# Output projection and MLP of an encoder trunk: the instruction order of VectorE, ScalarE and GpSimd written by hand instead of left to the scheduler

## The chip, the core and the metric

The kernel runs on one core of a Trainium2 chip. The core has TensorE (PE, matrix products, with a separate weight load PEld), VectorE (DVE), ScalarE (ACT), GpSimd (POOL) and SyncE (SP, which issues most transfers). Each works through its own queue of instructions in order, and waits where an instruction needs something that another engine has not finished. The metric is the device time of one execution in microseconds. Smaller is better.

## The reference

One encoder layer for 1280 tokens (256 of a prompt and 1024 of a sample), 1024 channels wide. Three token mixers feed a merged tensor, and from there:

```python
h  = h + merged @ w_o                                  # output projection, 1024 x 1024
hf = rmsnorm(h, norm_ff_g) @ w_ff1                     # first layer of the MLP, 1024 x 4096
h  = h + jnp.square(jax.nn.relu(hf)) @ w_ff2           # second layer, 4096 x 1024
pg = jax.nn.sigmoid(rmsnorm(h, norm_ple_g) @ w_ple_gate)
h  = h + (p @ w_ple_proj) * pg
return rmsnorm(h, final_norm_g)
```

All in float32. The change touches everything from the output projection to the second layer of the MLP, and the first statistics of the gate.

## The kernel before

Channels lie on the 128 partitions and tokens along the row; a tensor of 1024 channels is eight tiles of 128 x 1280. Every float32 factor is split in a high and a low part, and a product is three matmuls (high by high, high by low, low by high). Tokens are taken in two halves of 640, and a half is two matmuls of 320 columns, so one 128 x 128 block of weights against one half costs six matmuls of 128x320, and a tile of an output channel block (eight blocks of input) costs 48. PSUM tiles are of two banks (one half of 640 tokens).

**Output projection.** For each half, for each of eight output tiles: 48 matmuls, then `h_evac`: DVE adds the PSUM to the residual (L1182), ACT issues the store of `h` to HBM, ACT squares it (`hsq`, L1170) and DVE adds the square to a running sum (`hss`, L1171). In the first half the first two tiles are interleaved over the input blocks, since the last blocks of the merged tensor `mg` come late from the mixers. During the second half the first half is already normalised: `normed` multiplies `h` by the gain and by the row `rb` of the reciprocal norms (DVE, L1188), and `half_operand` makes its two parts (ACT copies the high part `xn`, L229, and DVE subtracts, L230).

**First layer.** A scheme with seven products in place of eight (P1 to P7) over token halves and channel halves. Its second operands are B11, B21, B22 and the differences T1 to T4, four tiles each, made in place from the normalised `h`. There are 16 pairs of output tiles, seven products each, of 24 matmuls (3.5 us). The weights of a product (`wx`) come from sums and differences of raw blocks (`wr`), each again split by ACT and DVE (`weight_split`). `evacuate` takes a product out of PSUM: by ACT after P1, P5, P6, and P4, by DVE (`add`, then a squared ReLU) after P2, P7 and P3. P6 and P7 add into the PSUM of P1, P3 into that of P5, and P4 into that of P1, so a later product of a chain waits until the earlier sum has been copied out. P1 and P2 of the first two pairs need only the first half of the tokens (B11, B21); P5, P6, P7 need T1, T2, T3, and with them the norms of the second half. Those come from `second_sums` (PE sums over partitions, L250; DVE scales, L257; POOL takes the power -1/2, L259) inside the first product and `second_rows` (PE spreads them out again, L1372, and ACT copies them to `rb`) inside the second.

**Second layer.** 56 steps: seven phases of eight, one phase for each product. A step is 48 matmuls into four PSUM tiles. For each step ACT and DVE make four operands (`tx` high and low for two halves, `whf` at L1452, `wlf` at L1453) out of reloaded activations `tr` and weights `wr`, one step ahead, with loads two steps ahead. At the end of a phase the four PSUM tiles are added to `h` by DVE. After three phases `half_square` follows each of them for the next norm, and after the fifth phase four more.

**What sets the order.** Inside `tc.manual_schedule(engines=...)` the engines named run instructions in the order in which the code writes them; other engines get their order from a scheduler, which places an instruction where it expects its inputs to be ready. SP is written by hand everywhere. Before, only PE is written by hand from the output projection to the second layer, and DVE, ACT and POOL are the scheduler's. The mixers ahead and the gate behind are written by hand on all four engines.

## Time and profile before

| | |
|---|---|
| median of 3 runs | 2097.21 us (2096.27 to 2097.41) |
| the profiled execution: own time | 2105.47 us |
| its span, first to last instruction | 2103.6 us |
| PE busy | 2023.4 us, 96% of the span |
| DVE, ACT, POOL busy | 1393.1, 607.5, 164.3 us |
| mean granted TensorE clock | 0.982 of full speed |

The profile is of one execution, 8 us above the median of the timed runs. Durations are read from it, and differences found in it are laid on the median. A row of a timeline can hold several instructions of one form (x2, x24); its duration then runs from the first start to the last end, and one instruction's end overlaps the next one's start by some 0.1 us, so that what an instruction costs its engine is the distance of starts.

### The profile page before, as it was taken

The numbers are of one execution on the slowest core, as the hardware profiler recorded it, in microseconds if no ns is written. First come the engines' busy times: TensorE is split into PE (matmuls) and PEld (weight loads), VectorE is DVE, ScalarE is ACT, GpSimd is POOL, SyncE is SP. The second block draws the span as 40 slices with busy tenths as digits, with TensorE's granted clock in tenths as the row PEclk, the third lists the DMA queues.
The fourth block names the chain that finished last, engine by engine and source line by source line (L and its number), as shares of the span: only waits on it lengthen the run. The fifth ranks groups of instructions, "written<-read, shape, count | busy, mean of one in ns | idle before, by whom it ended". The sixth has DMA issues, their size and how long they took to land.

```text
span 2103.6 us, 29411 instructions
## 1 busy us (share of the span) xinstructions
PE 2023.4 (96%) x12318; PEld 1882.8 (90%) x12318; DVE 1393.1 (66%) x1717; ACT 607.5 (29%) x820; POOL 164.3 (8%) x151
## 2 busy tenths in 40 slices
PE   8999999999999999999896899999989999999996
PEld 7888998888888888888796899999989999999896
DVE  5998328988888877537648766666556544477447
ACT  4423321111111136014233332223323333354213
POOL 1441000000000000005000000000000000000215
PEclk8999999999999999999998999999999999999998
DMA  7644431211111124744341333333467345454323
GB/s 263 256 175 173 142 105 65 66 56 56 65 66 59 49 100 170 265 154 158 132 161 72 128 128 128 134 135 134 152 241 297 110 132 177 161 178 139 110 94 134
DMA packets 84410, 290.32 MB, mean 138 GB/s; under 512 B 9251, under 2 KB 11654, under 8 KB 84278
## 3 DMA queue, kind: packets, MB, share of 16 engines
q1 hardware_dynamic: 69254, 233.09, 31.5%
q10 hardware_dynamic: 12416, 44.68, 5.6%
q0 software_dynamic: 2608, 10.68, 1.5%
q8 instruction: 96, 1.57, 0.3%
q14 instruction: 36, 0.29, 0.0%
HBM read 200.21 MB, written 88.20 MB: 137 GB/s over the span
## 4 chain that ended last, share of the span: by engine, by line
PE 90%; DVE 5%; DMA 2%; issue 1%; ACT 1%; POOL 1%; SPq 0%; POOLq 0%; DVEq 0%; ACTq 0%
PE mm L206 45%; PE z L206 37%; PE mm L1518 5%; PE mm L1032 1%; PE sm L971 1%; DVE h L1258 1%; DVE mg L230 1%; DMA cst<-in_cst 1%; DVE m L1017 0%; DVE xn L230 0%; DMA xT<-in_xT 0%; DVE h L1611 0%; PE sm L250 0%; DVE h L1188 0%; PE sm L975 0%
## 5 line engine op out<-in xcount | busy, mean ns | idle before, releaser
L206 PE MATMUL z<-xn,wx 128*128 128x320 f32 x2688 | 397.4, 310 | 22.6 <-DVE hx L1258 21.6
L206 PEld LDWEIGHTS z<-xn,wx 128*128 128x128 f32 x2688 | 396.4, 189 | 23.0 <-ACT xn L229 21.8
L206 PE MATMUL z<-tx,whf 128*128 128x320 f32 x1792 | 338.4, 311 | 10.8 <-ACT whf L1452 10.8
L206 PEld LDWEIGHTS z<-tx,whf 128*128 128x128 f32 x1792 | 283.9, 190 | 11.4 <-ACT whf L1452 11.4
L206 PE MATMUL mm<-xnh,wh 128*128 128x512 f32 (+1 forms) x1152 | 288.0, 358 | 0.0
L206 PE MATMUL mm<-xnh,wl 128*128 128x512 f32 (+1 forms) x1152 | 287.1, 358 | 0.0
L206 PE MATMUL mm<-xnl,wh 128*128 128x512 f32 (+1 forms) x1152 | 286.8, 357 | 0.0
L103 ACT ACTIVATE wh<-wr 128x1024 fp32r<-128x1024 f32 x80 | 84.7, 1059 | 576.8 <-PE mm L206 561.5
L206 PEld LDWEIGHTS mm<-xnh,wh 128*128 128x128 f32 x1152 | 190.9, 189 | 34.2 <-issue 0.2
L206 PEld LDWEIGHTS mm<-xnh,wl 128*128 128x128 f32 x1152 | 190.5, 189 | 33.9
L206 PEld LDWEIGHTS mm<-xnl,wh 128*128 128x128 f32 x1152 | 190.6, 189 | 33.7
L206 PE MATMUL z<-tx,wlf 128*128 128x320 f32 x896 | 206.4, 312 | 0.6 <-DVE wlf L1453 0.6
L807 DVE SCALAR_TENSOR_TENSOR acc<-vp,cst,acc 128x648 f32<-128x648 f32 x232 | 197.3, 893 | 0.0
L230 DVE TENSOR_TENSOR tx<-tr,tx 128x640 fp32r<-128x640 f32 x112 | 93.8, 843 | 146.8 <-ACT tx L229 146.4
L104 POOL TENSOR_TENSOR wl<-wr,wh 128x1024 fp32r<-128x1024 f32 x27 | 87.4, 3240 | 934.1 <-DVE wh L101 863.0
L206 PEld LDWEIGHTS z<-tx,wlf 128*128 128x128 f32 x896 | 150.7, 189 | 1.1 <-DVE wlf L1453 1.1
L229 ACT ACTIVATE tx<-tr 128x640 fp32r<-128x640 f32 x112 | 81.7, 733 | 224.5 <-PE z L206 160.1
L104 DVE TENSOR_TENSOR wl<-wr,wh 128x1024 fp32r<-128x1024 f32 x78 | 95.5, 1224 | 60.9 <-ACT wh L103 60.5
L1243 DVE TENSOR_TENSOR wx<-wr,wx 128x512 fp32r<-128x512 f32 x112 | 76.8, 688 | 87.3 <-ACT wx L1242 87.2
L206 PE MATMUL mm<-mg,wh 128*128 128x320 f32 x512 | 98.6, 314 | 10.6 <-ACT y L1064 7.2
L807 DVE SCALAR_TENSOR_TENSOR acc<-acc,pair_w 128x648 f32<-128x648 f32 x120 | 107.2, 894 | 0.0
L1242 ACT ACTIVATE wx<-wr 128x512 fp32r<-128x512 f32 x112 | 70.1, 628 | 123.6 <-PE z L206 107.5
(256 smaller groups left out, 2625.4 us busy)
## 6 DMA issues: line engine op xcount, KB each, us to landing
wr<-in_w_ff SPq DMA_DIRECT2D x80, 512.0 KB, 4.8
wr<-in_w_in SPq DMA_DIRECT2D x40, 512.0 KB, 4.2
tr<-d_t SPq DMA_DIRECT2D x32, 640.0 KB, 4.2
d_gate<-gt ACTq DMA_DIRECT2D x24, 640.0 KB, 2.9
tr<-d_b SPq DMA_DIRECT2D x24, 640.0 KB
gt<-d_gate SPq DMA_DIRECT2D x16, 640.0 KB, 9.1
d_b<-hy SPq DMA_DIRECT2D x32, 320.0 KB, 2.3
d_t<-ht SPq DMA_DIRECT2D x32, 320.0 KB, 2.2
```

The lines of the kernel that those rows point to most:

```text
L103: nc.scalar.activation(out=hi, in_=raw, func=AF.Copy)
L104: (nc.gpsimd if eng in "pq" else nc.vector).tensor_tensor(out=lo, in0=raw, in1=hi[:, :].bitcast(F32), op=ALU.subtract)
L206: ins = pe.matmul(ps[:, po:po + size], ww[:, wc:wc + P], xx[:, xo + xb:xo + xb + size], start=first and n == 0, stop=last and n == 2, skip ...
L229: act.activation(out=hi, in_=src, func=AF.Copy)
L230: eng.tensor_tensor(out=lo, in0=src, in1=f32(hi), op=ALU.subtract)
L807: dve.scalar_tensor_tensor(out=d[:, :HC], in0=x[:, s:s + HC], scalar=w, in1=d[:, :HC], op0=ALU.mult, op1=ALU.add)
L971: pe.matmul(out, u[:, uu + c0:uu + c0 + P], mw[:, mm:mm + 256], start=z == 0, stop=par == "o" and z == 2)
L1032: pe.matmul(out, t[:, off + ct * P:off + (ct + 1) * P], c, start=j == 0 and n == 0, stop=j == len(ts) - 1 and n == 2)
L1242: act.activation(out=hi, in_=src, func=AF.Copy)
L1243: dve.tensor_tensor(out=lo, in0=src, in1=f32(hi), op=ALU.subtract)
L1258: dve.tensor_tensor(out=out, in0=x, in1=y, op=op)
L1518: pe.matmul(ps[:, po:po + size], w[wn][:, K8[k]:K8[k] + P], XP[half][k][xn][:, xo:xo + size], start=k == 0 and n == 0, stop=k == KT - 1 an ...
```

## The change

1. The scope of the hand-written order: the second half of the output projection and both MLP layers now have PE, DVE, ACT and POOL in one `manual_schedule`. In the first half it is PE alone, as before.
2. The first half of the output projection interleaves three tiles instead of two, in PSUM tiles of the pool `z` that the MLP uses (opened earlier).
3. In the second half `normed` and `half_operand` of two tiles stand behind the evacuations of tiles 2 to 5; the first weights behind tiles 5 to 7. The gain of the second half's channels 4 to 7 is multiplied in by ACT (`second_scale`), and `rb` by POOL (`second_rows`) where DVE did both in one instruction.
4. In the first layer `evacuate` is taken out of `product`, and a table `behind` says for the first eight products in which order their evacuation, weights and operands are written. The order of products there is P5 P5 P6 P6 P7 P7 over the two pairs, where it was P5 P6 P5 P7 P6 P3 P7.
5. Loads and operands of the first steps of the second layer are issued within the last five products of the first (`ahead2`). The reloads of `h` are spread over two phases.
6. In the gate stage the statistics of the first norm are written ahead of the first product.

```diff
@@ output projection
+    def out_tile(i, half, x, w):
+        ps = z_psum()
+        for j in range(KT):
+            passes(ps, w, MG[half][j], K8[j], 0, HB, j == 0, j == KT - 1)
+        h_evac(i, half, ps, x)
+
     with tc.manual_schedule(engines={E.PE}):
-        for half in range(2):
...
-                if half and i >= 3:
-                    for k in {3: (0, 4), 4: (1, 5), 5: (2, 6), 6: (3, 7)}.get(i, ()):
-                        normed(k, 0)
-                        OPS["B21" if k > 3 else "B11"][k % 4] = half_operand(H[k][:, HALF[0]], "R", "xn")
...
+        pss = [z_psum() for _ in range(3)]
+        for k in range(KT + 4):
+            for n in range(3):
+                j = k - 2 * n
+                if 0 <= j < KT:
+                    passes(pss[n], ws[n], MG[0][j], K8[j], 0, HB, j == 0, j == KT - 1)
...
+    with tc.manual_schedule(engines={E.PE, E.DVE, E.Activation, E.Pool}):
...
@@ product
-            evacuate(i, n)
-        def second_sums():
...
-        for at, (i, n) in enumerate(sequence):
-            prepare(at + 1 + AHEAD)
-            hooks = {0: {3: second_sums}, 1: {2: second_rows}}.get(at, {})
-            product(i, n, made.popleft(), hooks)
@@ second half, first layer
+        for i in range(KT):
+            x = residual(i, 1)
+            out_tile(i, 1, x, W.next())
+            if i == 0:
+                rb = row_tile("rb")
+                r = token_rsqrt(ss, 0, NH)
+            if i == 1:
+                token_rows(r, rb, 0, NH)
+            for k in {2: (0, 4), 3: (1, 5), 4: (2, 6), 5: (3, 7)}.get(i, ()):
+                normed(k, 0)
+                OPS["B21" if k > 3 else "B11"][k % 4] = half_operand(H[k][:, HALF[0]], "R", "xn")
+            if 4 < i < 7:
+                prepare(2 * i - 8)
+            if 4 < i:
+                second_scale(i - 1)
+        prepare(6)
...
+            for k in range(4, KT):
+                h = H[k][:, HALF[1]]
+                pool.tensor_tensor(out=h, in0=h, in1=rb[:, HALF[1]], op=ALU.mult)
...
+        def operand(name, k):
+            b11, b12, b21, b22 = (h[:, c] for h in (H[k], H[k + 4]) for c in HALF)
+            if name == "T1":
+                normed(k, 1)
+                add(b11, b12, b11, ALU.subtract)
+                OPS[name][k] = half_operand(b11, "R", "xn")
...
+            elif name == "T3":
+                add(b12, b22, b12, ALU.subtract)
+                OPS[name][k] = half_operand(b12, "v" if k > 1 else "c", "xn")
+                add(b21, b21, b11, ALU.subtract)
...
+        behind = {0: (evacuate, 6), 1: ("T1 0", "T1 1", evacuate, "T1 2"), 2: (evacuate, "T1 3"),
+                  3: (evacuate, 8, "T2 0", "T2 1", "T2 2", "T2 3"), 4: (evacuate, 11, "T3 0", "T3 1"),
+                  5: (evacuate, 12, "T3 2", "T3 3"), 6: (evacuate, "B22 0", "B22 1", "B22 2", "B22 3"),
+                  7: (evacuate, 13, "T4 0", "T4 1", "T4 2", "T4 3")}
+        for at, (i, n) in enumerate(sequence):
+            product(i, n, made.popleft(), {0: {3: second_sums}, 1: {2: second_rows}}.get(at, {}))
+            left = len(sequence) - at
+            if left == 5:
+                ahead2(2, 0)
+            if left == 1:
+                ahead2(3, 2)
+            for step in behind.get(at, (evacuate, at + 6)):
...
+            if left == 2:
+                ahead2(3, 1)
@@ second layer
-            while loaded2 < min(n + 3, len(steps2)):
...
+            ahead2(n + 3, n + 2)
```

The first place is DVE between the last sum of squares of the second half (L1171) and the first scaling of T1 (L1188). `cmp` at L257 is what the norms of the second half wait for; `wr` and `wx` are first-layer weights. (`add` is L1258 before and L1247 now, `weight_split` on DVE L1243 and L1232.) Before:

```order
L1171 TENSOR_TENSOR hss_7697<-hss_7697,hsq_8727 128x640
L257 TENSOR_SCALAR cmp_8802<-z_8796 128x5
L1243 TENSOR_TENSOR wx_8809<-wr_1_8753,wx_8809 128x512
L1258 TENSOR_TENSOR wr_1_8753<-wr_1_8753,wr_0_8752 128x512
L1188 SCALAR_TENSOR_TENSOR h_7814<-h_7814,cst,rb_8324 128x640
```

Now:

```order
L1171 TENSOR_TENSOR hss_7702<-hss_7702,hsq_8764 128x640
L1247 TENSOR_TENSOR wr_8634<-wr_8634 128x512
L1232 TENSOR_TENSOR wx_8769<-wr_8634,wx_8769 128x512
L1247 TENSOR_TENSOR wr_8633<-wr_8634,wr_8633 128x512
L1247 TENSOR_TENSOR wr_8634<-wr_8634,wr_8633 128x512
L1247 TENSOR_TENSOR wr_1_8701<-wr_1_8701 128x512
L1232 TENSOR_TENSOR wx_8775<-wr_1_8701,wx_8775 128x512
L1247 TENSOR_TENSOR wr_0_8700<-wr_1_8701,wr_0_8700 128x512
L1247 TENSOR_TENSOR wr_1_8701<-wr_1_8701,wr_0_8700 128x512
L257 TENSOR_SCALAR cmp_8811<-z_8780 128x5
L1188 SCALAR_TENSOR_TENSOR h_7828<-h_7828,cst,rb_8277 128x640
```

Eight weight instructions, the weights of P5 for both pairs, stand ahead of `cmp` now; before there were none between the two.

The second place is ACT around the evacuation of the first pair's P6 into `hx` (L1326 before, L1315 now). `hy` is the evacuation of P5, `xn` the high part of an operand, `wx` of a weight. Before:

```order
L229 ACTIVATE xn_8906<-h_8133 128x640
L229 ACTIVATE xn_8881<-h_7814 128x640
L1324 ACTIVATE hy_9023<-z_8998 128x640
L229 ACTIVATE xn_8909<-h_8196 128x640
L1242 ACTIVATE wx_9025<-wr_1_8753 128x512
L1326 ACTIVATE hx_8806<-z_8771 128x640
L1242 ACTIVATE wx_9053<-wr_8743 128x512
L229 ACTIVATE xn_8886<-h_7818 128x640
```

Now (the four `xn` rows are T3, which is made by a subtraction on DVE ahead of each):

```order
L1313 ACTIVATE hy_8979<-z_8954 128x640
L1231 ACTIVATE wx_8981<-wr_8634 128x512
L1231 ACTIVATE wx_8984<-wr_1_8701 128x512
L1231 ACTIVATE wx_8988<-wr_8633 128x512
L229 ACTIVATE xn_8992<-h_7828 128x640
L229 ACTIVATE xn_8997<-h_7856 128x640
L1313 ACTIVATE hy_9026<-z_9001 128x640
L1231 ACTIVATE wx_9028<-wr_8634 128x512
L229 ACTIVATE xn_9032<-h_7874 128x640
L229 ACTIVATE xn_9037<-h_7949 128x640
L1315 ACTIVATE hx_8815<-z_8781 128x640
```

The evacuation of P6 now stands behind the high parts of all four T3 operands, and behind the evacuation of the second pair's P5.

The third place is DVE at the end of the second layer's fifth phase, from the third of its four evacuations to the weights `wlf` of the step after the next. `hss` sums squares; `hp` is an operand of the gate. Before:

```order
L1258 TENSOR_TENSOR h_12687<-z_14522,h_12687 128x640
L1466 SCALAR_TENSOR_TENSOR hp_15100<-h_12618,cst,hp_15100 128x640
L1171 TENSOR_TENSOR hss_12443<-hss_12443,hsq_14986 128x640
L1258 TENSOR_TENSOR h_12689<-z_14523,h_12689 128x640
L1171 TENSOR_TENSOR hss_12443<-hss_12443,hsq_15002 128x640
L230 TENSOR_TENSOR tx_15037<-tr_14944,tx_15037 128x640
L1171 TENSOR_TENSOR hss_12443<-hss_12443,hsq_15018 128x640
L230 TENSOR_TENSOR tx_15040<-tr_14944,tx_15040 128x640
L1171 TENSOR_TENSOR hss_12443<-hss_12443,hsq_15021 128x640
L1466 SCALAR_TENSOR_TENSOR hp_15103<-h_12756,cst,hp_15103 128x640
L1171 TENSOR_TENSOR hss_12443<-hss_12443,hsq_15024 128x640
L1453 TENSOR_TENSOR wlf_15118<-wr_15035,whf_15117 128x1024
```

Now:

```order
L1247 TENSOR_TENSOR h_12759<-z_14529,h_12759 128x640
L1171 TENSOR_TENSOR hss_12490<-hss_12490,hsq_15009 128x640
L1247 TENSOR_TENSOR h_12826<-z_14530,h_12826 128x640
L1171 TENSOR_TENSOR hss_12490<-hss_12490,hsq_15025 128x640
L1171 TENSOR_TENSOR hss_12490<-hss_12490,hsq_15028 128x640
L1171 TENSOR_TENSOR hss_12490<-hss_12490,hsq_15031 128x640
L1171 TENSOR_TENSOR hss_12490<-hss_12490,hsq_15034 128x640
L1171 TENSOR_TENSOR hss_12490<-hss_12490,hsq_15037 128x640
L230 TENSOR_TENSOR tx_15044<-tr_14951,tx_15044 128x640
L230 TENSOR_TENSOR tx_15047<-tr_14951,tx_15047 128x640
L1247 TENSOR_TENSOR wr_14953<-s_13017,wr_14953 128x1024
L1400 TENSOR_TENSOR wlf_15052<-wr_14953,whf_15051 128x1024
```

Before, the operands `tx` of that step stand between the sums of squares; now all seven sums stand ahead of `tx`, of the weights' sum `wr`, and so of `wlf`.

## Rows read from the trace of the kernel before

**Rows 1.** Parts 1 and 4 of the page: busy time, share and instruction count of an engine over the whole span, then the share of each engine in the chain of work that ended last.

```profile
PE 2023.4 (96%) x12318; PEld 1882.8 (90%) x12318; DVE 1393.1 (66%) x1717; ACT 607.5 (29%) x820; POOL 164.3 (8%) x151
...
PE 90%; DVE 5%; DMA 2%; issue 1%; ACT 1%; POOL 1%; SPq 0%; POOLq 0%; DVEq 0%; ACTq 0%
```

**Rows 2.** The waits of PE over the whole span, grouped: engine, tile and line that waited, whom it waited for, and then microseconds in total, times, longest.

```profile
PE z L206 <- DVE hx L1258: 21.6, 1, 21.6
PE z L206 <- ACT whf L1452: 10.8, 2, 9.7
PE mm L206 <- ACT y L1064: 7.2, 2, 6.8
...
PE sm L267 <- POOL cmr L259: 2.7, 2, 1.6
...
PE mm L1518 <- DVE pg L1525: 1.0, 1, 1.0
PE z L206 <- ACT wx L1242: 1.0, 1, 1.0
PE mm L1518 <- DVE h L1258: 1.0, 1, 1.0
...
PE z L206 <- DVE wlf L1453: 0.6, 1, 0.6
```

**Rows 3.** The timeline of PE, at the start of the output projection, at the change to the first layer, and at the change to the second layer: start in us, duration, engine, line and operation, tile written and read, shape, count in the row, and in brackets the idle time before it with its releaser.

```profile
1005.89 1.44 PE L206 MATMUL mm<-mg,wh 128*128 128x320 f32 x4 [6.76 <-ACT y L1064]
...
1009.06 0.74 PE L206 MATMUL mm<-mg,wh 128*128 128x320 f32 x4
...
1030.32 0.75 PE L206 MATMUL mm<-mg,wh 128*128 128x320 f32 x4
...
1031.20 0.75 PE L206 MATMUL mm<-mg,wh 128*128 128x320 f32 x4
...
1124.68 3.78 PE L206 MATMUL z<-xn,wx 128*128 128x320 f32 x24 [1.01 <-ACT wx L1242]
...
1162.84 3.34 PE L206 MATMUL z<-xn,wx 128*128 128x320 f32 x12 [21.55 <-DVE hx L1258]
1555.10 1.44 PE L206 MATMUL z<-tx,whf 128*128 128x320 f32 x4 [9.74 <-ACT whf L1452]
...
1558.52 0.75 PE L206 MATMUL z<-tx,whf 128*128 128x320 f32 x4
```

**Rows 4.** Windows of the trace: length, then the busy time of PE, PEld, DVE, ACT and POOL in it (with the number of instructions), the granted TensorE clock, the DMA share and GB/s.

```profile
1100.00:1123.00 23.00, 23.00 (x159) 23.00 (x158) 21.58 (x31) 9.58 (x14) 0.00 (x0) 1.00 0.44 164
1141.00:1163.00 22.00, 0.45 (x3) 0.21 (x3) 22.00 (x31) 8.83 (x13) 0.00 (x0) 0.60 0.00 0
1162.00:1166.00 4.00, 3.16 (x12) 3.19 (x13) 4.00 (x6) 0.05 (x1) 0.00 (x0) 0.52 0.22 86
1845.00:1860.00 15.00, 15.00 (x104) 15.00 (x103) 14.99 (x20) 11.15 (x17) 0.00 (x0) 1.00 0.43 124
```

**Rows 5.** The timeline of DVE around the first layer's entry, and one row from the end of the fifth phase of the second layer (columns as in rows 3).

```profile
1107.85 2.48 DVE L1188 SCALAR_TENSOR_TENSOR h<-h,cst,rb 128x640 f32<-128x640 f32 x3
...
1110.98 0.82 DVE L1182 TENSOR_TENSOR h<-mm,x 128x640 f32<-128x640 f32 x1
...
1118.39 1.28 DVE L1243 TENSOR_TENSOR wx<-wr,wx 128x512 fp32r<-128x512 f32 x2
...
1129.50 0.17 DVE L257 TENSOR_SCALAR cmp<-z 128x5 f32<-128x5 f32 x1 [2.31 <-PE z L250]
...
1139.51 0.82 DVE L1258 TENSOR_TENSOR h<-h 128x640 f32<-128x640 f32 x1
...
1161.86 0.83 DVE L1258 TENSOR_TENSOR hx<-z,hx 128x640 f32<-128x640 f32 x1
...
1174.27 0.82 DVE L230 TENSOR_TENSOR xn<-h,xn 128x640 fp32r<-128x640 f32 x1 [0.81 <-ACT xn L229]
...
1849.52 1.22 DVE L1453 TENSOR_TENSOR wlf<-wr,whf 128x1024 fp32r<-128x1024 f32 x1
```

**Rows 6.** The timeline of ACT in the same two places.

```profile
1112.20 0.74 ACT L1170 ACTIVATE hsq<-h 128x640 f32<-128x640 f32 x1 [0.22 <-ACT wx L1242]
...
1140.36 0.74 ACT L229 ACTIVATE xn<-h 128x640 fp32r<-128x640 f32 x1 [1.15 <-DVE h L1258]
...
1173.50 0.74 ACT L229 ACTIVATE xn<-h 128x640 fp32r<-128x640 f32 x1 [0.76 <-DVE wx L1243]
...
1844.06 1.04 ACT L1452 ACTIVATE whf<-wr 128x1024 fp32r<-128x1024 f32 x1
```

**Rows 7.** The timeline of POOL while the mixers end, and its one instruction at the first layer's entry.

```profile
994.57 6.39 POOL L1012 TENSOR_TENSOR y<-y,rl 128x1280 f32<-128x1280 f32 x2
1005.97 3.24 POOL L1012 TENSOR_TENSOR y<-y,rl 128x1280 f32<-128x1280 f32 x1 [5.01 <-ACT y L1064]
1129.75 1.72 POOL L259 TENSOR_TENSOR cmr<-cmp,cst 128x5 f32<-128x5 f32 x1 [46.59 <-DVE cmp L257]
```

**Rows 8.** The timeline of DVE over the end of the mixers, where POOL was at work beside it.

```profile
994.83 6.82 DVE L230 TENSOR_TENSOR mg<-m,mg 128x640 fp32r<-128x640 f32 x2
1001.57 1.48 DVE L1017 TENSOR_TENSOR m<-m,y 128x1280 f32<-128x1280 f32 x1
...
1006.34 4.22 DVE L1017 TENSOR_TENSOR m<-m,y 128x1280 f32<-128x1280 f32 x1
```

More of the change, by code (lines that the diff above doesn't have):

```diff
@@ L162, in sm_psum @@
     def sm_psum():
-        return psum_tile("sm")
+        return psum_tile("sm" if "sm" in psum else "z")
     def f32(ap):
@@ new lines, in out_tile @@
+    def out_tile(i, half, x, w):
[3 more added lines that the diff above has]
+        h_evac(i, half, ps, x)
+    with tc.manual_schedule(engines={E.PE}):
+        xs = [residual(i, 0) for i in range(3)]
+        ws = [W.next(2 - i) for i in range(3)]
+        pss = [z_psum() for _ in range(3)]
[4 more added lines that the diff above has]
+                    passes(pss[n], ws[n], MG[0][j], K8[j], 0, HB, j == 0, j == KT - 1)
+            if k - 7 in (0, 2, 4):
+                n = (k - 7) // 2
+                h_evac(n, 0, pss[n], xs[n])
+        for i in range(3, KT):
+            x = residual(i, 0)
+            out_tile(i, 0, x, W.next())
@@ new lines, in _trunk, with second_sums, second_rows @@
+        prepare(6)
+        stat_ps = z_psum()
+        def second_sums():
+            nonlocal r
+            for _ in token_sums(stat_ps, ss, NH, T):
+                pass
+            r = rsqrt_of(stat_ps, 5)
+        def second_rows():
+            for j in range(5):
+                c = 512 + j * P if j < 4 else P
+                pe.matmul(stat_ps[:, c:c + P], r[:, j:j + 1].to_broadcast([P, P]), ident, start=True, stop=True)
+            act.activation(out=rb[:, NH:NH + 512], in_=stat_ps[:, 512:1024], func=AF.Copy)
+            act.activation(out=rb[:, NH + 512:T], in_=stat_ps[:, P:2 * P], func=AF.Copy)
+            for k in range(4, KT):
+                h = H[k][:, HALF[1]]
+                pool.tensor_tensor(out=h, in0=h, in1=rb[:, HALF[1]], op=ALU.mult)
@@ new lines, in _trunk @@
+        behind = {0: (evacuate, 6), 1: ("T1 0", "T1 1", evacuate, "T1 2"), 2: (evacuate, "T1 3"),
[10 more added lines that the diff above has]
+            for step in behind.get(at, (evacuate, at + 6)):
+                if step is evacuate:
+                    evacuate(i, n)
+                elif isinstance(step, int):
+                    prepare(step)
+                else:
+                    name, k = step.split()
+                    operand(name, int(k))
+            if at == 0:
+                second_scale(7)
+            if left == 2:
+                ahead2(3, 1)
```

106 lines of the change are left out of this document (31 added, 75 removed).

## Prediction

> **What bounds the kernel now.** I read the page's shares first: PE is busy 96% of the span and takes 90% of the chain that ended last [rows 1]. The work of PE is the same in both kernels, so time moves only where PE waits or runs on a lower clock. Then PE's waits [rows 2], of which the change can reach these: 21.6 us at the entry of the first layer, 10.8 + 0.6 at the entry of the second, 6.8 at the start of the output projection, 1.0 for the first weights, and 2.7 + 1.0 + 1.0 at the start of the gate. A wait also costs clock: after 6.76 us of idling, 12 matmuls of 128x320 took 1009.06 - 1005.89 = 3.17 us [rows 3], against 1.76 at the usual 0.88 for six (1030.32 to 1031.20); after 21.55 us, 12 took 3.16 at a granted clock of 0.52 [rows 4]. That is 1.4 us on top each time, at the lower of the two clock levels (0.5 of 2.4 GHz). A tile of 48 matmuls is 7.03 us, a product of 24 is 3.51.
>
> The long wait has its cause in one row: DVE evacuates `hx` at 1161.86 [rows 5], after 22 us without a gap [rows 4], because the scheduler set 24 operand instructions ahead of it. So DVE is the second resource: full from 1100 to 1123 (21.58 of 23 us) and from 1141 to 1163.
>
> **Prices.** On DVE, from distances of starts in [rows 5]: an addition of 128x640 0.74, `normed` 0.80 (three in 2.48 with an overlap of 0.08), a weight half of 128x512 0.60, one of 128x1024 1.13 (estimate from its 1.22 less the overlap). From a DVE start to the ACT copy that needs it 0.85 (1139.51 to 1140.36) and from that copy to the subtraction that needs it 0.77 (1173.50 to 1174.27) [rows 5, 6]. In a written order DVE stands still through the ACT copy unless something else is written between. The code writes the operands one after another, so T2 costs 0.85 + 0.77 + 0.74 = 2.36 each (DVE busy 1.48), T3 with its second subtraction 3.1, T1 with `normed` and a dependent step 3.3, and an evacuation with squared ReLU 1.6.
>
> **A. Start of the output projection.** PE starts on the first PSUM tile when the last mixer tile is evacuated, at 1005.9 in both; before, 18 matmuls had run ahead of the wait. Three interleaved tiles need 144 matmuls = 21.1 us and 1.4 for the clock: done at 1028.4. Before, the third tile ends at about 1030.3 (the fourth begins at 1030.32 [rows 3]), since two tiles waited for late `mg`. **-1.9** (0 if the late tiles still catch three, -2.7 without a clock loss).
>
> **B. Entry of the first layer.** *Sums late.* Behind tiles 2 to 5 DVE now has the evacuation 0.74, a wait for ACT's store issue and square (1110.98 + 1.22 = 1112.20 [rows 6], then 0.8, so 1.3), the sum 0.74, two times `normed` + wait + subtraction 2.5, and a weight half of w_o with its wait 1.35: 9.1 us for a tile that PE does in 7.03. Four make 36.4; then two weight halves 1.2, tile 6's evacuation, square and sum with two weight halves 4.0, and tile 7's 2.8. The start is 1.1 late for the residual's load (estimate, 0 is possible). So the last sum is there 45.5 us after the end of tile 2. PE fills 5 x 7.03 + 3.5 of it, and 1.3 of waiting for the first weights: **L250 waits 4.4 to 5.6**; I take 4.4, the rounded terms being upper ends.
> *Norms late.* Between that sum and `cmp` now stand eight weight instructions (8 x 0.6 and two ACT trips of about 1.0: 6.8), then `cmp` and POOL 1.72 [rows 7]. PE has 18 matmuls and the column sums for 3.1 of 8.7: **5.6**. Before, `cmp` came at once after L250 and cost nothing.
> *T1.* Two T1 and the evacuation of P2 stand ahead of P5: 8.2 us from `rb`, against two products and a bit on PE, 0.9 of waiting. Beside it POOL now multiplies four tiles by `rb`. Rows say what that does: POOL 128x1280 is 3.0 to 3.2, so 1.5 for 640 [rows 7]; and a DVE instruction that ran into one, both inputs in SBUF, took 4.22 where it takes 1.48 [rows 8]. Four of 1.5 beside the first T1 let DVE through only in turns: 4.8 more. **P5 waits 5.7** (0.9 without a clash). The Trainium skill ("SBUF — State Buffer", Who interferes with whom) says that a DVE instruction with two SBUF inputs and a GpSimd instruction that reads SBUF exclude one another, the later one blocked for the whole instruction; the trace agrees (4.22 for 1.48), and by that rule too the ACT-to-POOL shift is no relief. The last T1 come 3.3 apart against 0.88 of PE per block, with an evacuation between: **4.7** more.
> *T2.* Four at 2.36 against 0.88: 1.48 each, less a little lead: **5.5**.
> *P7.* It needs P6 evacuated by ACT, and that row stands behind the four T3 copies. From the last T2 on DVE: four weight instructions and an ACT trip 3.3, three T3 9.4, 1.6 to the last copy, 0.6 for the copy and 0.8 for the evacuation = 15.7; PE has P6 of the second pair, 3.5: **11.9**.
> *Rest.* P4 waits 2.0 for P7's evacuation behind B22 and T4 on DVE; the third pair twice 3 for slots and evacuations still queued (walked the same way, 0 to 8 together): **8.3**.
> With 1.3 at the start that is 47.4, against 21.6 + 1.0 before: **+24.8**.
>
> **C. Entry of the second layer.** Loads are issued five products (17 us) ahead and the first two steps made ahead of the end; before, PE waited 10.8 + 0.6 from the last product to the second step. What is left is 1.6 for `wlf` behind the last evacuations. **-9.7** (-11.4 with nothing left; 0 if the loads wait for slots).
>
> **D. Phase ends of the second layer.** After the fifth phase DVE has from its first evacuation: four evacuations and seven sums 8.1, three waits for ACT's squares 2.9, four short ones 0.6, two `tx` 1.5, the sum for `wr` 1.1, ACT's `whf` 1.04 [rows 6] and two hops 0.3 = 15.5 until the step after the next can start. PE has that step's predecessor and the 1.7 left of the last one: 8.7. **6.8**, and 0.7 for `wlf`. After the sixth phase, with four squares fewer, 3.2 + 0.7. Before, the same stretch is full on both engines, PE 15.00 of 15 and DVE 14.99 [rows 4], with nothing lost, as `tx` and `whf` were set between. **+11.4**; 0 if the `tx` were early enough.
>
> **E. Start of the gate.** The sums wait now for the last DVE evacuations behind weight splits, 5.3, and the first gate product 4.2, 0.5 later: 10.0 against 4.7 in rows 2. The same working gives 7.9 for before, so it is 3.2 too high: **+3** (+2 to +5.3).
>
> **F. Clock.** Waits over 5 us: two of them before in the MLP (21.6, 9.7), now five (5.6, 5.7, 11.9, 6.8, 5.3), 1.4 each if 5.5 us costs what 6.76 did: +4.2; 0 if it costs nothing. **+2**.
>
> **Sum.** -1.9 + 24.8 - 9.7 + 11.4 + 3 + 2 = +29.6. In B and D some 40 handoffs are rounded up by up to 0.07, so I take off 2: +27.6. On the profiled execution 2105.5 would become 2133, on the median 2097.2 + 27.6 = **2124.8**.
>
> **The rivals.**
> *R1, no clash of POOL and DVE.* POOL's multiplications fall into DVE's waits for ACT. P5 waits 0.9 in place of 5.7, and one wait over 5 us goes: 2124.8 - 4.8 - 1.4 = 2118.6. Against it: 4.22 in rows 8.
> *R2, phase ends covered.* D is nothing if the operands stand two steps ahead in fact: 2124.8 - 11.4 - 1.4 = 2112. For it: 100% PE there before. Against it: now seven sums are written ahead.
> *R3, faster.* The wait of 21.6 came from one evacuation set behind 24 operand instructions; it now stands behind two. If DVE does not stand still for ACT (0.81 of idling before a subtraction in rows 5 is what it would have to hide), its own work up to P7 is about 22 us against 21 of products, so the first layer's entry costs some 4 + 1 in place of 22.6: -17.6; with A, C and a lost clock dip less, 2097.2 - 17.6 - 1.9 - 9.7 - 1.4 = 2067, or 2078 with D. It decides where B's waits sum to less than 22.6 + 11.6 - 14.4 - 2 = 18 us, D and E being as above.
> *R4, no loads ahead in effect.* The slots for `tr` come free only as the last products are evacuated: C is 0, 2134.5.
>
> **How the numbers follow.** The forecast 0.56, R1 0.13, R2 0.13, R4 0.06, R3 0.08, and 0.04 for a mixture that ends within 0.2% (4 us, about what a measurement of this kernel can tell from no change). The range goes from R2 with a few microseconds of B's rest taken away, 2107, to R4, 2137; outside stay R3, the mixture and little else. Faster 0.08, same 0.04, slower 0.88.
>
> **What would show it.** In PE's waits: the 21.6 behind `hx` L1258 gone, and in its place some 12 behind ACT `hx` L1315, two of 4 to 6 behind `hss` and `cmr`, one of 5 to 6 behind `hx` L1247, and a dozen short ones behind `xn`; `whf` (now L1399) no longer at the second layer's start but near its fifth and sixth phase ends, 7 and 3. DVE should show rows of over 2 us for 128x640 beside POOL L1452. The forecast is wrong if the wait behind L1315 is under 3 us, which would mean that T3 was done while PE still had products; or if no wait stands at the phase ends.

## The result and the profile after

The changed kernel takes 2120.01 us (median of 5 runs, 2112.73 to 2125.22), the one before 2097.41 in the same count (2096.27 to 2100.21): ratio 1.0099, 95% interval 1.0072 to 1.0126, so it is slower by 22.6 us. The forecast was 2124.8 in 2107 to 2137. The profiled execution has a span of 2120.3 us against 2103.6, but the start of the program, which the change does not touch, happened to be 3.7 us shorter in it: in the profiles of this document PE's restart in the output projection lies anywhere from 996.4 to 1007.1 us, and kernels with the same code up to there differ as well (1002.24 in the changed kernel, 996.43 in experiment 5). I therefore also compare what lies between the first matmul of the first layer and the end: 1001.4 us after (from 1118.92), 978.9 before (from 1124.68), which is 22.5 more.

PE's waits, grouped, in the changed kernel (columns as in [rows 2]):

```profile
PE z L206 <- ACT y L1064: 10.5, 1, 10.5
PE z L206 <- ACT hx L1315: 10.0, 1, 10.0
PE z L206 <- ACT whf L1399: 9.1, 2, 6.4
...
PE z L206 <- DVE hx L1247: 4.2, 1, 4.2
PE z L250 <- DVE hss L1171: 4.2, 1, 4.2
...
PE mm L1553 <- DVE h L1247: 3.2, 1, 3.2
PE z L206 <- ACT xn L229: 2.9, 4, 1.0
PE sm L250 <- DVE h L1247: 2.5, 1, 2.5
...
PE z L206 <- ACT hx L1305: 1.9, 1, 1.9
PE z L206 <- DVE hy L1247: 1.9, 1, 1.9
...
PE z L1447 <- POOL cmr L259: 0.7, 1, 0.7
```

The 21.6 behind `hx` and the 9.7 in front of the second layer [rows 2] are gone. In their place stand 10.0 behind ACT's `hx`, 4.2 twice, and a tail of waits of 0.7 to 2; then 6.4 and 2.7 behind `whf`, which in the timeline lie at 1858 and 1919, behind the second layer's fifth and sixth phase; then 2.5 and 3.2 at the start of the gate.

The group of the first layer's matmuls in the page (busy us, mean ns of one, then idle time before them), first of before, then of after:

```profile
L206 PE MATMUL z<-xn,wx 128*128 128x320 f32 x2688 | 397.4, 310 | 22.6 <-DVE hx L1258 21.6
```

```profile
L206 PE MATMUL z<-xn,wx 128*128 128x320 f32 x2688 | 410.3, 315 | 23.0 <-ACT hx L1315 10.0
```

The idle time is the same within 0.4 us, but the same 2688 matmuls are busy 12.9 us longer. Most of that is clock. With the column sums and rows that lie between them, PE is busy 15.2 us longer in this stage. It is busy for 27.5 us at a granted clock of 0.50, against 3.0 before; if half of such time is lost, that is 12 us (an estimate). The rest are blocks of six matmuls that short waits break up: from 1164.48 one takes 0.56 + 0.85 us, with a wait of 0.30 between, in place of the usual 0.88, and the granted clock is 1.00 there. The windows of after show where the clock was low (columns as in [rows 4]):

```profile
1110.00:1119.00 9.00, 8.58 (x59) 8.31 (x57) 6.09 (x8) 3.23 (x6) 0.00 (x0) 1.00 0.45 133
...
1127.00:1131.00 4.00, 3.77 (x16) 3.80 (x17) 3.21 (x6) 0.63 (x1) 0.00 (x0) 0.50 0.01 2
1131.00:1135.00 4.00, 3.50 (x14) 3.10 (x12) 2.12 (x5) 1.94 (x3) 1.06 (x1) 0.50 0.00 0
1135.00:1139.00 4.00, 3.84 (x16) 3.84 (x17) 0.50 (x1) 0.77 (x2) 0.56 (x2) 0.50 0.00 0
1139.00:1143.00 4.00, 4.00 (x28) 4.00 (x28) 3.86 (x2) 0.07 (x1) 4.00 (x3) 1.00 0.00 0
1151.00:1155.00 4.00, 4.00 (x16) 3.59 (x15) 3.16 (x5) 1.33 (x2) 0.00 (x0) 0.50 0.23 86
```

After the wait of 4.2 us for the sums, PE stays at the lower of its two clock levels (0.50) for 12 us, and falls to it again after the next wait of 4.2 (the window from 1151). By stage, from the ends and starts of PE's rows:

| stage | before | after | difference |
|---|---|---|---|
| PE's restart in the output projection (1005.89, 1002.24) to the first layer | 118.8 | 116.7 | -2.1 |
| first layer | 420.7 | 441.9 | +21.2 |
| wait in front of the second layer | 9.7 | 0 | -9.7 |
| second layer | 400.6 | 410.6 | +10.0 |
| gate and the rest | 147.9 | 148.9 | +1.0 |

The sum is +20.4; with the start's -3.7 it is the spans' +16.7.

The chain that sets the pace at the first layer's entry is on DVE (timeline of after, columns as in [rows 3]):

```profile
1126.26 0.82 DVE L1171 TENSOR_TENSOR hss<-hss,hsq 128x640 f32<-128x640 f32 x1 [1.17 <-ACT hsq L1170]
1127.00 0.69 DVE L1247 TENSOR_TENSOR wr<-wr 128x512 f32<-128x512 f32 x1
...
1133.71 0.15 DVE L257 TENSOR_SCALAR cmp<-z 128x5 f32<-128x5 f32 x1
1138.50 2.29 DVE L1188 SCALAR_TENSOR_TENSOR h<-h,cst,rb 128x640 f32<-128x640 f32 x1 [4.64 <-ACT rb L1449]
1140.83 2.07 DVE L1247 TENSOR_TENSOR h<-h 128x640 f32<-128x640 f32 x1
1143.70 1.30 DVE L230 TENSOR_TENSOR xn<-h,xn 128x640 fp32r<-128x640 f32 x1 [0.81 <-ACT xn L229]
1144.93 2.18 DVE L1188 SCALAR_TENSOR_TENSOR h<-h,cst,rb 128x640 f32<-128x640 f32 x1
...
1164.46 0.83 DVE L230 TENSOR_TENSOR xn<-h,xn 128x640 fp32r<-128x640 f32 x1 [0.80 <-ACT xn L229]
```

and beside it POOL, and the evacuation of P6 on ACT:

```profile
1138.54 7.89 POOL L1452 TENSOR_TENSOR h<-h,rb 128x640 f32<-128x640 f32 x4 [3.44 <-ACT rb L1449]
```

```profile
1184.40 0.74 ACT L229 ACTIVATE xn<-h 128x640 fp32r<-128x640 f32 x1 [2.41 <-DVE h L1247]
1185.05 0.69 ACT L1315 ACTIVATE hx<-z 128x640 f32<-128x640 f32 x1
```

The last sum ends at 1127.0, eight weight instructions follow, `cmp` at 1133.71, `normed` at 1138.50. The instructions beside POOL take 2.29, 2.07, 1.30 and 2.18 us where they take 0.88, 0.82, 0.83 and 0.88 alone: 4.4 us more. Each `xn` is preceded by 0.81 of standing still. The last T3 copy is at 1184.40, and the evacuation right behind it.

### The profile page after: what moved, and what is told of

Same layout as the page of the kernel before. It is cut to its first block, busy times and chain, and to the rows that moved or that the text cites. A ratio compares the mean times of both kernels' runs of the same rounds, so it can differ in the third digit from the quotient of the medians.

```text
span 2120.3 us, 29342 instructions
## 1 busy us (share of the span) xinstructions
PE 2035.5 (96%) x12318; PEld 1892.2 (89%) x12318; DVE 1403.2 (66%) x1713; ACT 616.4 (29%) x824; POOL 169.9 (8%) x155
## 5 line engine op out<-in xcount | busy, mean ns | idle before, releaser
L206 PE MATMUL z<-xn,wx 128*128 128x320 f32 x2688 | 410.3, 315 | 23.0 <-ACT hx L1315 10.0
L206 PEld LDWEIGHTS z<-xn,wx 128*128 128x128 f32 x2688 | 405.2, 192 | 27.6 <-ACT hx L1315 10.2
L1232 DVE TENSOR_TENSOR wx<-wr,wx 128x512 fp32r<-128x512 f32 x112 | 76.9, 689 | 109.5 <-ACT wx L1231 109.5
L206 PE MATMUL z<-mg,wh 128*128 128x320 f32 x512 | 97.4, 312 | 10.5 <-ACT y L1064 10.5
L1553 PE MATMUL mm<-hp,wh 128*128 128x384 f32 (+2 forms) x512 | 99.7, 317 | 7.1 <-DVE tk L1626 3.9
```

The lines of the kernel that those rows point to most:

```text
L206: ins = pe.matmul(ps[:, po:po + size], ww[:, wc:wc + P], xx[:, xo + xb:xo + xb + size], start=first and n == 0, stop=last and n == 2, skip ...
L1232: dve.tensor_tensor(out=lo, in0=src, in1=f32(hi), op=ALU.subtract)
L1553: pe.matmul(ps[:, po:po + size], w[wn][:, K8[k]:K8[k] + P], XP[half][k][xn][:, xo:xo + size], start=k == 0 and n == 0, stop=k == KT - 1 an ...
```

## The experiments

Each was measured against the kernel before, run beside it (its median was 2098.7, 2101.1 and 2100.4 in the three sessions). Its medians lie up to 3.7 us apart, so for effects of a few microseconds I give the time between the first layer's first matmul and the end in the profile as well (called the rest: 978.9 before, 1001.4 after). Each rest is from one profile and isn't exact to a microsecond either. Experiments 4 and 5 have the code of after up to the second layer, and their first layers took 441.8 and 439.1 us (after: 441.9). So a difference in the rest under some 3 us shows nothing by itself, and where an edit touches one stage I give that stage's time.

**1. Which part of the change gains: loads ahead alone, on the kernel before.**

```diff
             product(i, n, made.popleft(), hooks)
+            left = len(sequence) - at
+            if left == 5:
+                ahead2(2, 0)
+            if left == 2:
+                ahead2(3, 1)
+            if left == 1:
+                ahead2(3, 2)
```

> The kernel before, with one part of the change alone: the first loads and operands of the second layer are issued within the last five products of the first. My reading of the trace (term C): the 9.7 us in front of the second layer and the 1.7 us of slow matmuls behind it go, and nothing else moves: 10 to 12 us faster than before, about 2086, with no wait behind whf at the second layer's start and the 21.6 us behind hx as before. Rival (the gain of C in the change comes from the written order of DVE and ACT, not from the loads): the wait stays at 8 us or more, 2095 to 2098.

Measured 2085.5 (2083.3 to 2093.3), ratio 0.9939 [0.9917, 0.9960]; the rest 965.6, 13.3 less than before. In PE's timeline the last product runs into the second layer:

```profile
1533.81 12.80 PE L206 MATMUL z<-xn,wx 128*128 128x320 f32 x86
1546.45 0.75 PE L206 MATMUL z<-tx,whf 128*128 128x320 f32 x4
```

So term C is a gain of its own, and it needs no written order.

**2. The written order undone, everything else kept.**

```diff
-    with tc.manual_schedule(engines={E.PE, E.DVE, E.Activation, E.Pool}):
+    with tc.manual_schedule(engines={E.PE}):
```

> The changed kernel with one word undone: from the second half of the output projection to the second layer only PE is written by hand, and DVE, ACT and POOL go to the scheduler again; order of products, POOL's scaling, loads ahead, three tiles all stay. My theory (the loss comes from the written order, in which DVE stands still through every ACT copy, an evacuation stands behind operands, and sums stand ahead of the next step): first-layer waits fall from 28 us to about 12, the two waits at the phase ends (6.4 and 2.7) go, the loads ahead keep their gain: 2062 to 2075, faster than both. Rival 1 (POOL's scaling against DVE and the order of products are what costs): 2105 or more, with DVE rows of over 2 us. Rival 2 (low clock of PE after many short waits): 2095 to 2110, PE clock in the entry at 0.5 to 0.8 as now.

Measured 2067.8 (2067.6 to 2069.7), ratio 0.9848 [0.9820, 0.9876]: 52 us faster than the changed kernel, and faster than the one before by 31. PE's waits:

```profile
PE z L206 <- ACT xn L229: 5.0, 3, 2.3
...
PE z L206 <- DVE xn L230: 1.8, 2, 0.9
...
PE z L250 <- DVE hss L1171: 0.6, 1, 0.6
```

No wait behind `hx`, none behind `whf`. Over 80 us of the entry, PE and DVE of after, and then of this kernel (whose first layer begins 3.2 us earlier, at 1115.70):

```profile
1116.00:1196.00 80.00, 56.02 (x285) 51.27 (x285) 57.08 (x72) 30.34 (x48) 9.05 (x5) 0.79 0.06 21
```

```profile
1116.00:1196.00 80.00, 72.49 (x459) 70.45 (x458) 68.67 (x90) 35.67 (x57) 9.44 (x5) 0.94 0.24 88
```

DVE does 90 instructions in the window where the written order gets through 72, and PE 459 matmuls instead of 285. By stage, the first layer takes 411.1 us (441.9 in after), the second 395.1 (410.6), the gate and the rest 144.0 (148.9). The loss is the written order's; the rest of the change, taken together, is a gain.

**3. A good place in the code under the scheduler, alone, on the kernel before.** Operands behind the evacuations, as in the table `behind`, and the change's order of products.

```diff
-            evacuate(i, n)
...
+            for step in behind.get(at, ("",)):
+                if step:
+                    operand(step[:-2], int(step[-1]))
+                else:
+                    evacuate(i, n)
```

> The kernel before, DVE, ACT and POOL with the scheduler as there, with one part of the change alone: in the first layer the evacuations and the operands T1 to T4 are written in the change's sequence (table behind, products P5 P5 P6 P6 P7 P7), so that the operands stand behind the products' evacuations in the code instead of all inside the second product. My theory (the 21.6 us behind hx came from the place in the code, from which the scheduler takes its order among things that are ready; a good place under the scheduler is what makes 2068 possible): the 21.6 us go, 10 to 12 us of short waits behind xn come, 9 to 12 us faster than before, 2087 to 2090, with the 9.7 us behind whf still there. Rival (the scheduler moves the operands ahead of the evacuation whatever the code says, and three tiles and loads ahead made the 30 us): within 3 us of before, one wait of 15 us or more behind hx.

Measured 2089.3 (2085.7 to 2099.7), ratio 0.9948 [0.9933, 0.9963]; the rest 969.1, 9.8 less than before. The long wait is gone, the one in front of the second layer still there:

```profile
PE z L206 <- ACT whf L1458: 11.0, 2, 9.9
...
PE z L206 <- ACT xn L229: 4.6, 5, 2.7
```

So the 21.6 us came from the place of the operand instructions in the code. In DVE's timeline of before, 37 of them run between 1134.18 and the evacuation at 1161.86 (the prediction's 24 leave out the 13 subtractions that make low parts). The order of products changed too, but only from the sixth product on, and PE's long wait lies behind 96 matmuls, which are four products. How much of the 9.8 us the new order of products made afterwards, no run separates.

**4. The phase ends of the second layer (term D).**

```diff
-                        half_square(ss, H[4 * oh + m], th, m == 0 and name != "P3")
+                        if p == 6:
+                            half_square(ss, H[4 * oh + m], th, False)
+                        else:
+                            late.append((ss, H[4 * oh + m], th, m == 0))
...
+            for _ in range(2):
+                if late:
+                    half_square(*late.popleft())
```

> The changed kernel; the sums of squares behind the fifth and sixth phase later, as in the run that gave 2097.4, but those of the last phase left between its evacuations, as in the change. It splits that run's 22.6 us into terms D and E. My theory: D is the two waits (6.4 + 2.7), 0.4 and 1.5 to 2 us of slow matmuls, 10 to 12 us, so 2108 to 2110 here, and E, the waits of 2.5 and 3.2 us at the start of the gate with the clock behind them, the other 8 or so, which stay. Rival (the whole gain is D, for instance through the clock over a long stretch behind it): 2097 to 2100.

Measured 2105.6 (2104.0 to 2113.5), ratio 1.0031 [1.0018, 1.0044]; the rest 990.5, 10.9 less than after. The second layer takes 399.3 us in place of 410.6, and the first 441.8, as in after; so term D is worth 11.3. The median fell by 14.4, more than expected.

**5. The same, and the last phase's sums behind all its evacuations.**

```diff
-                        half_square(ss, H[4 * oh + m], th, m == 0 and name != "P3")
+                        late.append((ss, H[4 * oh + m], th, m == 0 and name != "P3"))
...
+            if p == 6 and tp == 7:
+                while late:
+                    half_square(*late.popleft())
```

> The changed kernel; the sums of squares behind the fifth and sixth phase of the second layer are written two by two behind the operands of the following steps instead of all at once ahead of them. My theory (term D: the step after the next waits for its tx and whf, which stand behind seven sums on DVE): the waits of 6.4 and 2.7 us behind whf go, with the slow matmuls after the first of them; at most some waits of 0.5 us in the following steps: 8 to 11 us faster than the changed kernel's 2120, about 2110. Rival (the operands wait for their loads or for slots there, not for the sums): the two waits stay, 2118 to 2122.

Measured 2097.4 (2095.7 to 2105.1), ratio 0.9992 [0.9976, 1.0007]; the rest 979.9, 21.4 less than after. That is twice what I expected, since I had counted only the fifth and sixth phase. Experiment 4, made afterwards, splits it. The second layer takes 399.3 us here too, so 11.3 are those phases'. The gate and the rest take 141.5 in place of 148.9, 7.4 less, and of the waits of 2.5 and 3.2 only this is left:

```profile
PE mm L1560 <- DVE h L1247: 0.2, 1, 0.2
```

The other 2.8 us lie in the first layer, which this edit does not touch.

**6. Does DVE stand still for ACT? Operands in groups.**

```diff
+            for k in ks:
+                b11, b12, b21, b22 = q[k]
...
+                elif name == "T2":
+                    add(b11, b22, b11, ALU.subtract)
...
+            for k in ks:
+                b11, b12, b21, b22 = q[k]
+                if name in ("T1", "T2"):
+                    OPS[name][k] = half_operand(b11, "R", "xn")
```

> The changed kernel, all written by hand as there; only that neighbouring operands of one name are written in groups: first the subtractions of all of them on DVE, then their high and low parts, so that DVE works on the next tile while ACT copies. My theory (in the written order DVE stands still 0.8 us for each ACT copy): T2 0 to 3 take 6 instead of 9.4 us, the T3 pairs 5 instead of 6.3 each; the 10.0 us behind hx L1315 fall to 5 to 6, the waits behind the T2 xn merge into one of 1 to 2 us, P5 starts as before; 7 to 10 us faster than the changed kernel, about 2111. Rival (DVE's own work is the limit, ACT copies are hidden anyway): 2118 to 2121.

Measured 2109.0 (2105.6 to 2110.7), ratio 1.0042 [1.0027, 1.0056]; the rest 992.8, 8.6 less than after. The wait behind `hx` L1315 is 7.1 in place of 10.0, a little more than expected, and the waits behind `xn` in T2 are one of 1.6. The first layer takes 432.4 us, 9.4 less. So standing still for ACT cost some 9 us.

**7. The evacuation's place or DVE's pace? T3 written behind the evacuation of P6.**

```diff
-                  3: (evacuate, 8, "T2 0", "T2 1", "T2 2", "T2 3"), 4: (evacuate, 11, "T3 0", "T3 1"),
-                  5: (evacuate, 12, "T3 2", "T3 3"), 6: (evacuate, "B22 0", "B22 1", "B22 2", "B22 3"),
+                  3: (evacuate, 8, "T2 0", "T2 1", "T2 2", "T2 3"), 4: (evacuate, 11),
+                  5: (evacuate, 12), 6: (evacuate, "T3 0", "T3 1", "T3 2", "T3 3", "B22 0", "B22 1", "B22 2", "B22 3"),
```

> The changed kernel; the four T3 operands are written behind the evacuation of the first pair's P6 instead of ahead of it, so that ACT can empty that PSUM as soon as P6 ends. Reading 1 (the prediction's words: P7 waits since the evacuation stands behind the T3 copies): the 10.0 us go, 6 to 8 us faster, 2112 to 2114. Reading 2 (DVE's chain of T3 sets the time at which P7 can go through its four blocks, whatever stands on ACT): the 10.0 us behind hx L1315 go, but four waits of 1.7 + 0.6 us behind xn come in their place and a small one for the second pair; 2117 to 2122, no change within the spread. I lean to reading 2.

Measured 2116.9 (2114.9 to 2118.8), ratio 1.0078 [1.0058, 1.0097]; the rest 1001.1, 0.3 less than after; the first layer takes 440.8 in place of 441.9. PE's waits:

```profile
PE z L206 <- ACT xn L229: 6.6, 8, 1.4
...
PE z L206 <- ACT hx L1315: 0.8, 1, 0.8
```

The 10.0 behind `hx` are 0.8 now, and those behind `xn` went from 2.9 to 6.6, with slow matmuls between them. Reading 1 forecast a gain of 6 to 8 us, which isn't there. Reading 2 holds: the row that PE waited for was the last in the line, and not the cause.

**8. Is the low clock a loss of its own? PE kept busy through the wait for the sums.** 28 matmuls that nobody reads.

```diff
+            for j in range(28):
+                pe.matmul(stat_ps[:, :320], OPS["B11"][3][0][:, :P], OPS["B11"][3][0][:, :320], start=True, stop=True)
             for _ in token_sums(stat_ps, ss, NH, T):
```

> The changed kernel; 28 more matmuls of 128x320 (4.1 us), whose result nobody reads, stand in the wait of 4.2 us ahead of the column sums of the second half, so that PE works on through it. Rival (PE's low clock after that wait, 0.50 over the next 12 us, is a loss of its own): the clock stays at 1.00, the products behind it take 2.6 instead of 5.2 us, and the kernel is 4 to 6 us faster than the changed one. My theory (DVE sets the pace there, the slow matmuls only fill what would be a wait): the products are faster, but the wait for cmr grows from 0.7 to 3 to 5 us, and P5 starts at the same time within 1 us; the time stays at 2118 to 2121 within the spread.

Measured 2117.4 (2115.8 to 2120.5), ratio 1.0084 [1.0054, 1.0113]; the rest 1000.9, 0.5 less than after. PE's timeline, of after and of this kernel:

```profile
1127.23 2.26 PE L250 MATMUL z<-cst,hss 128*128 128x1 f32 x10 [4.17 <-DVE hss L1171]
1129.36 5.15 PE L206 MATMUL z<-xn,wx 128*128 128x320 f32 x18
1135.16 2.50 PE L1447 MATMUL z<-cst,cmr 128*128 128x128 f32 x10 [0.66 <-POOL cmr L259]
...
1150.48 4.95 PE L206 MATMUL z<-xn,wx 128*128 128x320 f32 x16 [4.23 <-DVE hx L1247]
```

```profile
1121.14 1.28 PE L250 MATMUL z<-cst,hss 128*128 128x1 f32 x10
1122.28 2.88 PE L206 MATMUL z<-xn,wx 128*128 128x320 f32 x18
1129.15 2.44 PE L1449 MATMUL z<-cst,cmr 128*128 128x128 f32 x10 [3.99 <-POOL cmr L259]
...
1144.42 5.46 PE L206 MATMUL z<-xn,wx 128*128 128x320 f32 x18 [4.35 <-DVE hx L1247]
```

18 matmuls take 2.88 instead of 5.15, and the wait for `cmr` grows from 0.66 to 3.99. From the column sums to P5 it is 23.25 us in after and 23.28 here. So the low clock of these 18 matmuls costs nothing: it fills time in which PE would have waited for DVE.

That does not hold for all that is slow there. The ten matmuls that spread the norms out as rows (L1447, here L1449) lie in the path to T1, since ACT copies their result to `rb` and DVE's first `normed` waits for it. They ran at half clock in both kernels, 2.50 and 2.44 us. In experiment 5, with the code of after up to there, they ran faster:

```profile
1122.26 2.26 PE L250 MATMUL z<-cst,hss 128*128 128x1 f32 x10 [4.16 <-DVE hss L1171]
...
1130.18 1.38 PE L1447 MATMUL z<-cst,cmr 128*128 128x128 f32 x10 [1.03 <-POOL cmr L259]
...
1144.37 5.18 PE L206 MATMUL z<-xn,wx 128*128 128x320 f32 x18 [4.84 <-DVE hx L1247]
```

There it is 22.11 us from the column sums to P5, 1.1 less, which is what those ten matmuls were faster. On the way of the engine that sets the pace, the low clock does cost time.

**9. The norms ahead of the weights of P5.**

```diff
-        prepare(6)
         stat_ps = z_psum()
```

> The changed kernel; the weights of P5 are written behind the first product instead of ahead of it, so that cmp (L257) comes at once behind the column sums, as before the change. The prediction's price of that step was 5.6 us. By the trace of the changed kernel the wait was 0.7 and PE ran at half clock. My theory: the norms come 6 us earlier, but the eight weight instructions then stand between cmp and T1, so that T1 starts about 3 to 4 us earlier and the rest follows: 2 to 4 us faster, 2116 to 2118. Rival (the step is worth its full price): 5 to 7 us faster, 2113 to 2115. Other rival (nothing, as PE waits for POOL's multiplications in any case): 2119 to 2121.

Measured 2115.8 (2114.7 to 2117.4), ratio 1.0070 [1.0048, 1.0092]; the rest 998.1, 3.3 less than after. From the column sums to P5 it is 20.98 us (1124.09 to 1145.07) against 23.25. But the ten matmuls of L1447 took 1.28 us here and 2.50 in after; against the 22.11 of experiment 5, where they took 1.38, it is 1.1. The step is worth 1 to 2 us there, not 5.6: the eight weight instructions now stand between `cmp` and T1, from 1126.57 to 1133.21. The 3.3 of the rest are too near to the 2.7 by which first layers of the same code differ to say more.

**10. POOL's share, under the scheduler.** ACT's multiplication by the gain goes with it; DVE does both in one instruction again.

```diff
-            for k in range(4, KT):
-                h = H[k][:, HALF[1]]
-                pool.tensor_tensor(out=h, in0=h, in1=rb[:, HALF[1]], op=ALU.mult)
...
             elif name == "T2":
+                normed(k + 4, 1)
```

> The changed kernel with DVE, ACT and POOL left to the scheduler from the second half on (2067.8 measured), and in it rb multiplied in on DVE again with the gain, without POOL and without ACT scaling. My theory (POOL's four multiplications lock out DVE for about 4 us just where PE waits for T1, while four products on DVE cost 0.8 each later): 1 to 4 us faster, 2064 to 2067, with no DVE instruction of 128x640 over 1 us in the entry. Rival (the shift to POOL is a relief of the full DVE): 1 to 3 us slower, 2069 to 2071.

Measured 2066.4 (2061.4 to 2067.0), ratio 0.9829 [0.9805, 0.9854]; against 2067.8 the medians do not settle 1.4 us, and of the 3.5 between the rests, 946.7 and 950.2, only 1.9 lie in the first layer. DVE at the same place, with POOL and without:

```profile
1125.95 4.39 DVE L1188 SCALAR_TENSOR_TENSOR h<-h,cst,rb 128x640 f32<-128x640 f32 x2 [3.86 <-ACT rb L1449]
1130.27 4.27 DVE L1247 TENSOR_TENSOR h<-h 128x640 f32<-128x640 f32 x2
```

```profile
1128.58 1.68 DVE L1188 SCALAR_TENSOR_TENSOR h<-h,cst,rb 128x640 f32<-128x640 f32 x2 [3.90 <-ACT rb L1447]
1130.17 1.56 DVE L1247 TENSOR_TENSOR h<-h 128x640 f32<-128x640 f32 x2
```

Four instructions take 8.5 us beside POOL and 3.1 without. For DVE's instructions the clash is clear. That the kernel gains by its going is what I expected, but not shown: the difference lies within the spread. By its median this is the fastest version, 1.7% under the kernel before.

**11. All repairs together, by hand.** Experiments 5, 6, 9 and the DVE multiplication of 10 in the changed kernel, with the written order kept; of each its first line:

```diff
-                        half_square(ss, H[4 * oh + m], th, m == 0 and name != "P3")
...
-        def operand(name, k):
+        def operands(name, ks):
...
-        prepare(6)
...
-                pool.tensor_tensor(out=h, in0=h, in1=rb[:, HALF[1]], op=ALU.mult)
```

> The changed kernel, all written by hand, with five repairs: sums of squares of the second layer two by two behind the next operands and, in the last phase, behind all evacuations; the weights of P5 behind the first product instead of ahead of the norms; rb multiplied in on DVE again (no POOL, no ACT scaling); operands written in groups. My theory (the loss is a sum of places where the written order makes DVE wait or puts late work first): 2120 - 22.6 (sums, as measured) - 4 (norms earlier) - 1 (POOL) - 8 (groups) = 2084 to 2090, faster than the kernel before and slower than the scheduler's 2068. Rival (a hand-written order of these engines costs as such, about as much as now): 2095 or more.

Measured 2086.9 (2084.4 to 2088.4), ratio 0.9934 [0.9914, 0.9953]; the rest 968.1, 33.3 less than after. By stage that is 14.6 in the first layer, 11.3 in the second and 7.5 in the gate and the rest. The parts measured one by one (21.4, 3.3, 8.6) add up to the same 33.3 without POOL's, but each may be off by some 3 us, so that they agree so closely is chance. A written order is not slow as such, but it stays 20 us behind the scheduler's here (experiment 10, also without POOL's multiplications): PE still waits 4.2 for `hss`, 5.5 for `hx` and 4.0 for `xn`.

## Why the prediction held, point by point

The direction, the places and the total held (+27.6 forecast, +22.6 measured). The terms:

- **A** -1.9: measured -2.1 up to the first product, of which 0.6 is the shorter wait for the first weights (0.42 for 1.01) that the prediction has in B. The three tiles ran without a further wait from 1002.24 on.
- **B** +24.8 as waits: **mis-sized in its make-up**. The stage lost 21.2, but the waits in it rose by only 5.8 (27.4 against 21.6), and the rest is matmuls that take longer: 12.9 in the first layer's products and 2.3 in the column sums and rows. Most steps were there, each shorter than forecast: the last sum 4.2 late (4.4 forecast), POOL's clash 4.4 (4.8), P5 waiting 4.2 (5.7), the last T1 1.3 (4.7), T2 3.2 (5.5), P7 10.0 (11.9; by its own terms, 15.7 less 3.5, it would be 12.2). Two steps failed. "Norms late", 5.6, was a wait of 0.7, since PE went through the 18 matmuls and the column sums at half clock (5.15 + 2.26 us instead of about 2.9 + 1.2) and so arrived later (with the fill of experiment 8 the wait is 4.0); experiment 9 puts its worth at 1 to 2. And for P7 the prediction named the evacuation behind the four T3 copies; experiment 7 shows that DVE's chain of T3 sets the time and the evacuation's place costs nothing that shows. "The rest", 8.3, was 3.9 (1.95 + 1.90).
- **C** -9.7: the size held, by a reading that was wrong in part. Of the 10.8 + 0.6 of before, only 9.7 lie at the entry; the other two waits are 59 us behind it:

```profile
1614.43 0.86 PE L206 MATMUL z<-tx,whf 128*128 128x320 f32 x4 [1.09 <-ACT whf L1452]
...
1615.94 0.56 PE L206 MATMUL z<-tx,wlf 128*128 128x320 f32 x2 [0.65 <-DVE wlf L1453]
```

  At the entry the change leaves 1.4 for `wlf` (1.6 forecast), so 8.3 are gained there. The two later waits are gone as well, but not through the loads ahead, since experiment 1 still has them (1.1 and 0.6). Alone, the loads gained 13.1 by the medians (slow matmuls behind the waits go too).
- **D** +11.4: two waits of 6.4 and 2.7 with 0.4 for `wlf`, where 6.8 and 3.2 with 0.7 each were forecast. The mechanism held, and with the slow matmuls behind the waits the whole is 11.3 (experiment 4).
- **E** +3: measured +1.0 (5.7 of waits against 4.7). The place was right; but it holds more than either kernel shows, 7.4 when the sums leave it (experiment 5).
- **F** +2: **the term that failed**. Lower clock took some 12 us of PE's time in the first layer alone (the estimate above). I had charged 1.4 us for each long wait, on top of the waits. After a wait of 4.2 us the clock stayed low for 12 us, and where 18 of those matmuls ran, this time came out of a wait instead of being added to it; for the ten on DVE's path 1.1 was added (experiment 8). For the other slow stretches no run tells the two apart. In the first layer B and F are therefore one sum of 21.2, and not 24.8 of waits with a little clock. B's waits were forecast 19 us too high, and 15 us of longer matmuls were left out of it; that the two nearly cancel is luck, but for the part that experiment 8 shows.
- **R1** was wrong: the clash was there, and measured at 4.4. The Trainium skill's rule ("SBUF — State Buffer", Who interferes with whom) agrees with the rows: 2.29 for 0.88 beside POOL, and nothing of it without (experiment 10). **R2** was wrong (experiment 4), and **R4** (C was full). **R3** had the mechanism right and the place wrong: a better place of the evacuations does remove the 21.6 (experiment 3), but the time comes near R3's 2067 only in the runs where the scheduler orders DVE (2067.8 in experiment 2); with DVE standing still for ACT in the written order, other waits take its place.

The changed kernel's five runs lie 12.5 us apart, those of before 3.9. Their mean clocks differ too (0.975 for 2125.2, 0.982 for 2112.7); why one execution stays low longer than another no run here settles. One side sum of the prediction does not come out: A without a clock loss would be -1.9 - 1.4 = -3.3, not -2.7; the forecast does not use it.

## What to carry to other kernels

A written order on an engine that hands work to another and takes it back should hold the next tile's work between the two; one operand at a time cost 0.8 us of standing still each, and grouping alone gave some 9. When a scheduler is at hand, the place of instructions in the code is worth moving first (9.8 us, with an order of products to match) and fixing the order last (it cost 52). And before a wait is charged, ask who sets the pace there: the row a wait is put down to can be moved away and the wait stays under other names (experiment 7), and a lower clock costs nothing where it only fills a wait, but it does on the path that others wait for (1.1 us for ten matmuls, experiment 8).

## What had not been expected

PE's granted clock stayed at 0.50 for about 12 us (1127 to 1139) after a wait of only 4.2 us, while PE was busy 11.1 of them; after 21.6 us of waiting in the kernel before it was back at 1.00 within 4 us, as the window behind the one in [rows 4] shows:

```profile
1166.00:1170.00 4.00, 4.00 (x30) 4.00 (x29) 2.92 (x5) 2.59 (x4) 0.00 (x0) 1.00 0.21 82
```

In experiment 5, with the same code up to there, it was back at 1.00 by 1130, 8 us after PE's restart at 1122.26. In the kernel with the fill it did not fall at that wait, but behind the longer wait for `cmr` that came in its place (2.44 us for the ten matmuls of L1449), and the rest did not change by more than 0.5 us.
